# Adding U to the residual on VectorE in every round, and issuing two weight loads with the last slab of the round before

## The chip, the cores and the metric

The kernel runs on one core of one Trainium2 chip. The metric is the device time of one execution in microseconds. Before the change the median of three runs is 1344.67 us (1343.59 to 1345.03).

## What is computed

Two layers of a decoder over 512 tokens of width 1024, in float32. Each layer is a mixer (attention in layer 0, a gated recurrence in layer 1) and then an MLP with a squared ReLU, each behind an RMSNorm and added to the residual stream x. The change lies in the MLP alone, with `w1` of 1024 x 4096 and `w2` of 4096 x 1024:

```python
def squared_relu_mlp(h, w1, w2):
    a = jax.nn.relu(h @ w1)
    return (a * a) @ w2

    ...
        h = rmsnorm(x, norm_gains[layer, 1])
        x = x + squared_relu_mlp(h, mlp_w1[layer], mlp_w2[layer])
```

## The kernel before

The residual stays in SBUF for the whole program, as two tiles `xt[0]` and `xt[1]` (the left and the right half of the columns), each with four blocks of 128 tokens. Float32 products are made of three matmuls: each operand is split into a high part that TensorE takes at full rate and the rest, and high x high, high x low and low x high are added up in PSUM.

**Slabs.** Weights come through a plan, a list of pieces in the order in which TensorE uses them. A piece of `w1` (`full`, 256 columns) is loaded in two halves by SP's DMA queue (`wr`, three buffers, L259). ScalarE casts each half to `wh` (L266), VectorE subtracts to get `wl` (L267). There are two slabs' worth of `wh` and `wl`, and the next slab is always prepared one ahead. So a cast waits until TensorE has left a buffer, and a load waits until the split of an earlier half has freed its `wr`.

**Rounds.** An MLP is four rounds, q = 0 to 3. In a round, four slabs of `w1` (two products of 24 matmuls each, `gemm_w`) give 1024 of the 4096 hidden columns, which `Seven.take` squares and splits. Then a 1024 x 1024 block of `w2` is applied by Strassen's scheme in Winograd's form: seven products of half size instead of eight (`seven_products`). Its four quarters B11, B12, B21, B22 are loaded raw (`load` in `seven`, L288, two DMAs of 512 KB each), and the sums that the scheme needs are made in place, by a negation on ScalarE (`flip`, L294) and an accumulating DMA on GpSimd's queue (L295, L324). Each of the seven slabs is then split by ScalarE (`wh`, L302) and VectorE (`wl`, L303). B12's buffers hold T1 and then T2 later in the round; B12 and B22 share a pool of four buffers (tag R4).

**The seven products** run in this order: a11, s1, a12, s4, s2, s3, a22. Each is two tiles of 12 x 2 matmuls into PSUM, alternating between the pools `mm` and `z`, with two banks each. The first tile's product a11 is kept in `U[t]`, s2's product is added to it (p6, L827), and s3's as well (p7, L832). The residual takes U after s2 (one block) and after s3 (two blocks). The function `back` (L710) is VectorE's addition to `xt`. For the additions of U the kernel before uses `add`: in the last round of an MLP it is `back`, and in the other three a DMA on GpSimd's queue that accumulates into `xt` (L824):

```python
        def add(h, t, u):
            if last:
                back(h, t, u)
            else:
                nc.gpsimd.dma_start(out=xt[h][:, t, :], in_=u, accum_op=ALU.add)
```

After a22 the blocks `xt[0][:, 2 + t]` take that product by `back` as well (p4), which frees its bank of `mm`. The next round's first matmuls (`gemm_w` of the first slab of `w1`) go into the banks of `mm` too.

TensorE's order is that of the program. On the other engines and on the queues a scheduler sets the order when the program is built; each engine and queue then works in order and waits on semaphores.

Of the kernel before, what the change touches and what calls it, by code (L numbers as in the profile page):

```python
# [13 lines left out]
ALU = mybir.AluOpType  # L14
# [3 lines left out]
D = 1024  # L18
# [4 lines left out]
SLAB = 256  # L23
FF = 4 * D
# [35 lines left out]
def trunk(  # L60
# [17 lines left out]
    nc = tc.nc  # L78
# [13 lines left out]
    def sb(tag, shape=(P, S), dt=F32, name=None):  # L92
        pool = gp if tag in "PQ" else ap
        return pool.tile(list(shape), dt, tag=tag, bufs=BUFS[tag], name=name or tag)

    def ps(tag, shape=(P, S), name=None):
        return pp.tile(list(shape), F32, tag=tag, bufs=PB[tag], name=name or f"ps_{tag}")

    def f(t):
        return t.bitcast(F32)  # L100
# [78 lines left out]
    def gain(layer, j, kt):  # L179
# [15 lines left out]
        out=later[:, 3 * P :], in_=later[:, 3 * P :], pattern=[[-1, P]], compare_op=ALU.is_gt,  # L195
# [4 lines left out]
        out=before[:, P:], in_=before[:, P:], pattern=[[1, P]], compare_op=ALU.is_gt,  # L200
# [70 lines left out]
    def seven(w, r0):  # L271

        b = {}

        def rows(i, j, a):
            r = r0 + i * (D // 2) + a * 2 * P
            return w[r : r + 2 * P, j * S : (j + 1) * S].rearrange("(k p) c -> p k c", p=P)

        def load(i, j):

            tag = {(0, 0): "B", (1, 0): "X5", (0, 1): "R4", (1, 1): "R4"}[i, j]
            shape = (P, 10 * P) if tag == "X5" else (P, TT, SLAB)
            b[i, j] = []
            for a in range(2):
                t = sb(tag, shape, name="raw")
                t = t if tag == "X5" else t.rearrange("p t c -> p (t c)")
                t = t[:, : 2 * S].rearrange("p (k c) -> p k c", c=S)
                nc.sync.dma_start(out=t, in_=rows(i, j, a))  # L288
                b[i, j].append(t)

        def flip(at, plus):

            for a in range(2):
                nc.scalar.mul(b[at][a], b[at][a], -1.0)  # L294
                nc.gpsimd.dma_start(out=b[at][a], in_=plus(a), accum_op=ALU.add)  # L295

        def slab(at):
            hi = wp.tile([P, KT // 2, S], F32R, tag="wh", bufs=2, name="wh")
            lo = wp.tile([P, KT // 2, S], F32R, tag="wl", bufs=2, name="wl")
            for a in range(2):  # L300
                c = slice(2 * a, 2 * a + 2)
                nc.scalar.copy(hi[:, c, :], b[at][a])  # L302
                nc.vector.tensor_tensor(  # L303
                    out=lo[:, c, :], in0=b[at][a], in1=f(hi[:, c, :]), op=ALU.subtract
                )
            return hi, lo

        def b12():
            load(0, 1)

        def b11():
            load(0, 0)

        def t1():
            flip((0, 1), lambda a: rows(0, 0, a))
            load(1, 1)

        def b21():
            load(1, 0)

        def slab_t1():
            got = slab((0, 1))
            for a in range(2):
                nc.gpsimd.dma_start(out=b[0, 1][a], in_=rows(1, 1, a), accum_op=ALU.add)  # L324
            flip((0, 0), lambda a: b[0, 1][a])
            return got

        def slab_b21():
            got = slab((1, 0))
            flip((1, 0), lambda a: b[0, 1][a])  # L330
            return got

        slabs = [
            lambda: slab((0, 0)), slab_t1, slab_b21, lambda: slab((1, 1)), lambda: slab((0, 1)),
            lambda: slab((0, 0)), lambda: slab((1, 0)),
        ]
        return [("load", g) for g in (b12, b11, t1, b21)], [("slab", g) for g in slabs]

    class Weights:
        def __init__(self, plan):  # L340
# [24 lines left out]
    def full(w, r0, c0):  # L365
        return (w, r0, KT, c0, SLAB)
# [10 lines left out]

    def plan_mlp(layer):
        got = []
        for q in range(FF // D):  # L380
            loads, slabs = seven(mlp_w2[layer], q * D)
            for c in range(4):
                got += [full(mlp_w1[layer], 0, q * D + c * SLAB), loads[c]]
            got += slabs
        return got

    plan += plan_project(sb_w_o[0]) + plan_mlp(0)
    for hp in range(4):
        plan += [full(hg_w_in[0], 0, n * D + hp * SLAB) for n in range(4)]
    plan += plan_project(hg_w_o[0]) + plan_mlp(1)  # L390
    weights = Weights(plan)

# [33 lines left out]
    xt = [cp.tile([P, TT, S], F32, name=f"xt{h}") for h in range(2)]  # L426
# [282 lines left out]
    def back(h, t, p, op=ALU.add):  # L709
        nc.vector.tensor_tensor(out=xt[h][:, t, :], in0=xt[h][:, t, :], in1=p, op=op)  # L710

    def chain(o, wsl, acts):

        hi, lo = wsl
        n = len(acts)
        for k, (ah, al) in enumerate(acts):
            mm(o, ah, hi[:, k, :], k == 0, False)
            mm(o, ah, lo[:, k, :], False, False)
            mm(o, al, hi[:, k, :], False, k == n - 1)
            yield  # L720
# [75 lines left out]
            }[name]  # L796
            return [[blk(x, at + t) for x in pair] for pair in src]

    def seven_products(A, done, last):


        U = []

        def p1(t, p):
            U.append(sb("AT", name="U"))
            nc.scalar.copy(U[t], p)  # L806
            back(0, t, p)

        def p2(t, p):
            back(0, t, p)  # L810
            done(0, t)

        def p5(t, p):
            back(1, t, p, ALU.subtract)
            back(1, 2 + t, p, ALU.subtract)

        def p3(t, p):
            back(1, t, p)

        def add(h, t, u):  # L820
            if last:
                back(h, t, u)
            else:
                nc.gpsimd.dma_start(out=xt[h][:, t, :], in_=u, accum_op=ALU.add)  # L824

        def p6(t, p):
            nc.vector.tensor_add(U[t], U[t], p)  # L827
            add(1, t, U[t])
            done(1, t)

        def p7(t, p):
            nc.vector.tensor_add(U[t], U[t], p)  # L832
            add(1, 2 + t, U[t])
            done(1, 2 + t)
            add(0, 2 + t, U[t])

        def p4(t, p):
            back(0, 2 + t, p, ALU.subtract)
            done(0, 2 + t)

        steps = [
            ("a11", p1), ("s1", p5), ("a12", p2), ("s4", p3), ("s2", p6), ("s3", p7), ("a22", p4),
        ]
        for n, (name, then) in enumerate(steps):
            wsl = weights.next()
            for t in range(2):
                p = ps("z" if n % 2 else "mm", name="ps_mm")
                yield from chain(p, wsl, A.part(name, t))
                then(t, p)

    def mlp(norm, nxt=None):
        task = line.spawn(norm.finish())
        rounds = FF // D
        for q in range(rounds):
            A = Seven()
            for c in range(4):
                wsl = weights.next()
                if q + c == 0:
                    early = yield from two(wsl, norm)
                    yield [task]  # L860
                for j in range(2):
                    if q + c == 0:
                        p = early[j]
                    else:
                        p = ps("mm")
                        yield from gemm_w(p, wsl, j, norm.acts)
                    u = sb("sq", name="u")
                    nc.vector.scalar_tensor_tensor(  # L868
                        out=u, in0=p, scalar=0.0, in1=norm.R, op0=ALU.max, op1=ALU.mult
                    )  # L870
                    A.take(u)

            def done(h, t):
                if q < rounds - 1:
                    return
                if nxt is None:
                    nc.sync.dma_start(
                        out=out[0, t * P : (t + 1) * P, h * S : (h + 1) * S], in_=xt[h][:, t, :]
                    )
                    return  # L880
                nxt.squares(h, t)
                if t == TT - 1:
                    nxt.turn(h, LAG["x7"] if h else LAG["x"])

            yield from seven_products(A, done, q == rounds - 1)


    def hgrn(norm):
# [292 lines left out]
    for c in range(4):  # L1181
        for j in range(2):
            k = 2 * c + j
            nc.sync.dma_start(
                out=xt[k // 4][:, :, (k % 4) * P : (k % 4 + 1) * P],
                in_=x[0, :, k * P : (k + 1) * P].rearrange("(t p) c -> p t c", p=P),
            )
            if j == 0:
                i = 2 * (c % 2)
                nc.sync.dma_start(  # L1190
                    out=start["raws"][c // 2][:, i : i + 2, :],
                    in_=w0[r0 + 2 * c * P : r0 + 2 * (c + 1) * P, c0 : c0 + SLAB].rearrange(
                        "(k p) c -> p k c", p=P
                    ),
# [61 lines left out]
```

## Time and profile before

| | before |
|---|---|
| median of 3 runs | 1344.67 us |
| profiled execution, its own time | 1343.56 us |
| span of that execution | 1341.9 us |
| mean granted clock of TensorE | 0.981 |
| TensorE busy | 1273.8 us, 95% |
| VectorE busy | 933.5 us, 70% |
| ScalarE busy | 611.6 us, 46% |
| DMA queue of SP (hardware) | 109.22 MB, 25.1% of 16 engines |
| DMA queue of GpSimd (software) | 43.31 MB, 18.4% of 16 engines |
| accumulating DMAs xt<-U | 36 of 256 KB, median 6.0 us to landing |

The profile is of one execution. PE is TensorE, DVE is VectorE, ACT is ScalarE, POOL is GpSimd, SP is the engine that issues most DMAs. In a row of the timeline stand the start and the length in us, the engine, the line, the operation, what is written and read, and in brackets how long the engine was idle before it and who released it. Matmuls are pipelined: the length of one (0.39 us) is more than the distance from one to the next. Layer 0's MLP rounds 1, 2, 3 begin at 403.69, 494.56 and 586.87 us, layer 1's at 1069.20, 1161.98 and 1253.84 us. "Boundary" means the change from one round to the next, so there are three in each MLP, six in all.

### The profile page before, as it was taken

To read this page: it belongs to the slowest core of one execution; us is meant where nothing else is said; L and a number is where in the kernel's file an instruction comes from. 1 tells how busy PE (TensorE), PEld (TensorE's weight loads), DVE (VectorE), ACT (ScalarE), POOL (GpSimd) and SP (SyncE) were. 2 spreads that over 40 slices of the span, in tenths; PEclk is the share of its full clock that TensorE was granted. 3 is DMA by queue.
4 is the path that set the end of the run, shared out by engine and by line. 5 is a ranking of instruction groups with operands and counts; after the bars stand their busy time and mean duration, and the time that the engine had idled before them with its cause. 6 is when DMAs were issued, how large, how long until landed. Compare 5 with 4: busy or idle time off the path is not lost. (4 is left out here: it accounts for less than half of the span.)

```text
span 1341.9 us, 17978 instructions
## 1 busy us (share of the span) xinstructions
PE 1273.8 (95%) x6817; PEld 1079.9 (80%) x6817; DVE 933.5 (70%) x1763; ACT 611.6 (46%) x991; POOL 178.4 (13%) x239
## 2 busy tenths in 40 slices
PE   8999999999989989989999999999999799899798
PEld 7989898778867868768878888888888688687687
DVE  4787687856854846746878888787668457467476
ACT  5555454534733624625552324342446345355262
POOL 1000001000120120210113132232001201203101
PEclk8999999999999989989999999999999899899899
DMA  6312124223394592771532212226424936828615
GB/s 186 95 34 62 38 74 126 95 82 91 73 245 137 94 242 88 165 197 63 96 93 64 90 53 78 63 79 167 132 82 87 256 95 144 217 63 190 186 23 135
DMA packets 109687, 153.68 MB, mean 115 GB/s; under 512 B 5432, under 2 KB 71136, under 8 KB 109600
## 3 DMA queue, kind: packets, MB, share of 16 engines
q1 hardware_dynamic: 91024, 109.22, 25.1%
q0 software_dynamic: 18576, 43.31, 18.4%
q8 instruction: 54, 0.88, 0.3%
q14 instruction: 33, 0.27, 0.1%
HBM read 124.19 MB, written 2.10 MB: 94 GB/s over the span
## 5 line engine op out<-in xcount | busy, mean ns | idle before, releaser
L154 PE MATMUL ps_mm<-xh,wh 128*128 128x512 f32 x592 | 237.9, 402 | 35.5 <-DVE xt L710 35.5
L154 PE MATMUL ps_mm<-xl,wh 128*128 128x512 f32 x592 | 235.2, 397 | 0.0
L154 PE MATMUL ps_mm<-xh,wl 128*128 128x512 f32 x592 | 235.1, 397 | 0.0
L266 ACT CAST wh<-wr 128x1024 fp32r<-128x1024 f32 x134 | 136.4, 1052 | 173.4 <-PE ps_mm L154 123.1
L154 PE MATMUL ps_mm<-wh,xh 128*128 128x256 f32 x592 | 173.5, 293 | 0.0
L154 PE MATMUL ps_mm<-wl,xh 128*128 128x256 f32 x592 | 167.7, 283 | 2.1 <-DVE wl L544 2.1
L267 DVE TENSOR_TENSOR wl<-wr,wh 128x1024 fp32r<-128x1024 f32 x134 | 162.1, 1231 | 9.1 <-ACT wh L266 8.9
L154 PE MATMUL ps_mm<-wh,xl 128*128 128x256 f32 x592 | 167.6, 283 | 0.0
L154 PEld LDWEIGHTS ps_mm<-xh,wh 128*128 128x128 f32 x592 | 114.5, 193 | 61.4 <-issue 37.9
L303 DVE TENSOR_TENSOR wl<-raw,wh 128x1024 fp32r<-128x1024 f32 x112 | 132.7, 1220 | 37.4 <-ACT wh L302 37.3
L710 DVE TENSOR_TENSOR xt<-xt,ps_mm 128x512 f32<-128x512 f32 x128 | 86.0, 682 | 83.1 <-PE ps_mm L154 47.3
L154 PEld LDWEIGHTS ps_mm<-xh,wl 128*128 128x128 f32 x592 | 114.0, 193 | 24.4
L154 PEld LDWEIGHTS ps_mm<-xl,wh 128*128 128x128 f32 x592 | 114.3, 193 | 23.3
L302 ACT CAST wh<-raw 128x1024 fp32r<-128x1024 f32 x112 | 111.4, 1047 | 44.0 <-PE ps_mm L154 40.4
L154 PEld LDWEIGHTS ps_mm<-wh,xh 128*128 128x128 f32 x592 | 113.4, 192 | 4.1 <-issue 3.6
L154 PEld LDWEIGHTS ps_mm<-wl,xh 128*128 128x128 f32 x592 | 113.5, 192 | 2.8 <-DVE wl L544 2.3
L154 PEld LDWEIGHTS ps_mm<-wh,xl 128*128 128x128 f32 x592 | 113.5, 192 | 0.0
L324 POOL DMA_DIRECT2D raw<-in_mlp_w_dram x16 | 19.5, 1247 | 546.5 <-DVE wl L303 546.0
L868 DVE SCALAR_TENSOR_TENSOR u<-ps_mm,R 128x512 f32<-128x512 f32 x60 | 41.4, 689 | 66.2 <-PE ps_mm L154 66.2
L294 ACT ACTIVATE raw<-raw 128x1024 f32<-128x1024 f32 x48 | 50.7, 1059 | 38.7 <-DMA raw<-in_mlp_w_dram 38.7
L667 DVE TENSOR_TENSOR_SCAN sn<-sn,later 128x128 f32<-128x128 f32 (+3 forms) x64 | 51.2, 816 | 8.4 <-ACT sn L664 7.4
L154 PE MATMUL ps_mm<-wl,s31h 128*128 128x512 f32 x128 | 51.7, 404 | 4.2 <-DVE wl L303 4.2
(236 smaller groups left out, 2543.8 us busy)
## 6 DMA issues: line engine op xcount, KB each, us to landing
raw<-in_mlp_w_dram SPq DMA_DIRECT2D x64, 512.0 KB, 7.5
wr<-in_mlp_w_dram SPq DMA_DIRECT2D x64, 512.0 KB, 4.7
raw<-in_mlp_w_dram POOLq DMA_DIRECT2D x32, 512.0 KB, 6.3
raw<-raw POOLq DMA_DIRECT2D x32, 512.0 KB, 5.8
wr<-in_hg_w_in_dram SPq DMA_DIRECT2D x32, 512.0 KB, 3.8
wr<-in_sb_w_qkv_dram SPq DMA_DIRECT2D x22, 512.0 KB, 3.8
xt<-U POOLq DMA_DIRECT2D x36, 256.0 KB, 6.0
wr<-in_sb_w_o_dram SPq DMA_DIRECT2D x8, 512.0 KB, 3.9
```

What stands on the lines that cost most here:

```text
L154: nc.tensor.matmul(o, lhsT=lhsT, rhs=rhs, start=start, stop=stop, **kw)
L266: nc.scalar.copy(hi[:, c, :], raw)
L267: nc.vector.tensor_tensor(out=lo[:, c, :], in0=raw, in1=f(hi[:, c, :]), op=ALU.subtract)
L294: nc.scalar.mul(b[at][a], b[at][a], -1.0)
L302: nc.scalar.copy(hi[:, c, :], b[at][a])
L303: nc.vector.tensor_tensor(out=lo[:, c, :], in0=b[at][a], in1=f(hi[:, c, :]), op=ALU.subtract)
L324: nc.gpsimd.dma_start(out=b[0, 1][a], in_=rows(1, 1, a), accum_op=ALU.add)
L667: nc.vector.tensor_tensor_scan(out=rev, data0=rev, data1=later[:, S - W :][:, ::-1], initial=1.0, op0=ALU.mult, op1=ALU.max,)
L710: nc.vector.tensor_tensor(out=xt[h][:, t, :], in0=xt[h][:, t, :], in1=p, op=op)
L868: nc.vector.scalar_tensor_tensor(out=u, in0=p, scalar=0.0, in1=norm.R, op0=ALU.max, op1=ALU.mult)
```

## The change

U is added to the residual by `back`, so by VectorE, in all rounds: `add` and its DMA go, 36 of them (six at each boundary). And the load steps of a round are put together differently. Before: B12, B11, then the negation and accumulation that make T1 together with the load of B22, then B21, one after each `w1` slab. After: B12 and B22 are one step, `early`, which stands ahead of the last slab of the round before (in an MLP's first round, behind its first `w1` slab), then B11, B21 and T1 stand between the `w1` slabs.

```diff
-        def b12():
+        def early():
             load(0, 1)
-
-        def b11():
-            load(0, 0)
+            load(1, 1)
 
         def t1():
             flip((0, 1), lambda a: rows(0, 0, a))
-            load(1, 1)
-
-        def b21():
-            load(1, 0)
...
-        return [("load", g) for g in (b12, b11, t1, b21)], [("slab", g) for g in slabs]
+        steps = (early, lambda: load(0, 0), lambda: load(1, 0), t1)
+        return [("load", g) for g in steps], [("slab", g) for g in slabs]
...
     def plan_mlp(layer):
         got = []
-        for q in range(FF // D):
-            loads, slabs = seven(mlp_w2[layer], q * D)
-            for c in range(4):
-                got += [full(mlp_w1[layer], 0, q * D + c * SLAB), loads[c]]
-            got += slabs
+        rounds = [seven(mlp_w2[layer], q * D) for q in range(FF // D)]
+        for q, ((early, *loads), slabs) in enumerate(rounds):
+            w1 = [full(mlp_w1[layer], 0, q * D + c * SLAB) for c in range(4)]
+            got += w1[:1] + ([] if q else [early])
+            for slab, step in zip(w1[1:], loads):
+                got += [step, slab]
+            got += slabs[:-1] + [r[0][0] for r in rounds[q + 1 : q + 2]] + slabs[-1:]
         return got
...
-        def add(h, t, u):
-            if last:
-                back(h, t, u)
-            else:
-                nc.gpsimd.dma_start(out=xt[h][:, t, :], in_=u, accum_op=ALU.add)
-
         def p6(t, p):
             nc.vector.tensor_add(U[t], U[t], p)
-            add(1, t, U[t])
+            back(1, t, U[t])
             done(1, t)
 
         def p7(t, p):
             nc.vector.tensor_add(U[t], U[t], p)
-            add(1, 2 + t, U[t])
+            back(1, 2 + t, U[t])
             done(1, 2 + t)
-            add(0, 2 + t, U[t])
+            back(0, 2 + t, U[t])
```

How this moves instructions is seen in the order in which they stand on each engine. VectorE before, at the end of the first round of layer 0, from s2's U to the splits of the second `w1` slab (`xt_99` is `xt[0]`, `xt_100` is `xt[1]`):

```order
L827 TENSOR_TENSOR U<-U,ps_mm 128x512 x2
L303 TENSOR_TENSOR wl<-raw,wh 128x1024 x2
L832 TENSOR_TENSOR U<-U,ps_mm 128x512 x2
L267 TENSOR_TENSOR wl<-wr,wh 128x1024 x2
L710 TENSOR_TENSOR xt_99<-xt_99,ps_mm 128x512 x2
L267 TENSOR_TENSOR wl<-wr,wh 128x1024 x2
```

VectorE now, at the same place, from the addition of s2's second U on (lines are three to nine lower in the changed text, so `back` is L707):

```order
L707 TENSOR_TENSOR xt_100<-xt_100,U 128x512
L303 TENSOR_TENSOR wl<-raw,wh 128x1024 x2
L823 TENSOR_TENSOR U<-U,ps_mm 128x512
L707 TENSOR_TENSOR xt_100<-xt_100,U 128x512
L707 TENSOR_TENSOR xt_99<-xt_99,U 128x512
L823 TENSOR_TENSOR U<-U,ps_mm 128x512
L707 TENSOR_TENSOR xt_100<-xt_100,U 128x512
L707 TENSOR_TENSOR xt_99<-xt_99,U 128x512
L267 TENSOR_TENSOR wl<-wr,wh 128x1024
L707 TENSOR_TENSOR xt_99<-xt_99,ps_mm 128x512
L267 TENSOR_TENSOR wl<-wr,wh 128x1024
L707 TENSOR_TENSOR xt_99<-xt_99,ps_mm 128x512
```

Each U is followed by its additions, six per boundary, and a22's first `back` stands behind one split of the first `w1` slab instead of two. Nothing else moves on VectorE; the orders of TensorE and ScalarE do not change, and on GpSimd's queue only the DMAs xt<-U are gone.

SP's queue before, at the boundary from the first to the second round of layer 0. The numbers tell the loads apart: raw_4101 and 4103 are the next round's B12, 4265 and 4267 its B22, 4181 and 4183 its B11, 4367 and 4369 its B21; wr_4107 and 4111 are the halves of its second `w1` slab:

```order
L259 DMA wr_4107<-in_mlp_w1_dram 128x4x256
L288 DMA raw_4101<-in_mlp_w2_dram 128x2x512
L288 DMA raw_4103<-in_mlp_w2_dram 128x2x512
L288 DMA raw_4265<-in_mlp_w2_dram 128x2x512
L288 DMA raw_4267<-in_mlp_w2_dram 128x2x512
L288 DMA raw_4181<-in_mlp_w2_dram 128x2x512
L288 DMA raw_4183<-in_mlp_w2_dram 128x2x512
L288 DMA raw_4367<-in_mlp_w2_dram 128x2x512
L288 DMA raw_4369<-in_mlp_w2_dram 128x2x512
L259 DMA wr_4111<-in_mlp_w1_dram 128x4x256
```

SP's queue now, at the same place. Here raw_4025 and 4027 are B12, 4029 and 4031 B22, 4109 and 4111 B11, 4189 and 4191 B21; wr_4115 and 4119 are the halves of the second `w1` slab:

```order
L259 DMA wr_4115<-in_mlp_w1_dram 128x4x256
L288 DMA raw_4025<-in_mlp_w2_dram 128x2x512
L288 DMA raw_4027<-in_mlp_w2_dram 128x2x512
L288 DMA raw_4029<-in_mlp_w2_dram 128x2x512
L288 DMA raw_4031<-in_mlp_w2_dram 128x2x512
L288 DMA raw_4109<-in_mlp_w2_dram 128x2x512
L288 DMA raw_4111<-in_mlp_w2_dram 128x2x512
L288 DMA raw_4189<-in_mlp_w2_dram 128x2x512
L288 DMA raw_4191<-in_mlp_w2_dram 128x2x512
L259 DMA wr_4119<-in_mlp_w1_dram 128x4x256
```

Only the names have changed: the loads of B12, B22, B11 and B21 stand in this order, behind the first half of the second `w1` slab, in both.

4 lines of the change are left out of this document (2 added, 2 removed).

## The prediction

> **What bounds the kernel now.** I read the page first, for the engine that is busiest, then the waits of TensorE, then the chain of waits, and then, round by round, TensorE's own timeline and its clock.
>
> ```profile
> PE 1273.8 (95%) x6817; PEld 1079.9 (80%) x6817; DVE 933.5 (70%) x1763; ACT 611.6 (46%) x991; POOL 178.4 (13%) x239
> ```
>
> TensorE (PE) is the bound: it is busy 95% of the 1341.9 us span. So a change to VectorE (DVE) or to the DMA queues is worth what it takes out of TensorE's idle time, or out of its slow time. TensorE's waits, by total (engine, line, who was waited for: us, times, longest):
>
> ```profile
> PE ps_mm L154 <- DVE xt L710: 36.5, 7, 7.3
> PE ps_mm L154 <- DVE wl L303: 4.2, 6, 0.8
> PE ps_mm L154 <- ACT wh L302: 2.0, 4, 0.9
> ```
>
> The first row is by far the largest wait of TensorE: for VectorE's `back` (L710), which adds a product in PSUM to the residual. TensorE's timeline shows where. These are the first matmuls of rounds 1, 2 and 3 of each MLP, with the idle time ahead of each in brackets:
>
> ```profile
> 403.69 0.77 PE L154 MATMUL ps_mm<-xh,wh 128*128 128x512 f32 x1 [6.43 <-DVE xt L710]
> 494.56 0.76 PE L154 MATMUL ps_mm<-xh,wh 128*128 128x512 f32 x1 [4.72 <-DVE xt L710]
> 586.87 0.77 PE L154 MATMUL ps_mm<-xh,wh 128*128 128x512 f32 x1 [5.94 <-DVE xt L710]
> 1069.20 0.77 PE L154 MATMUL ps_mm<-xh,wh 128*128 128x512 f32 x1 [6.47 <-DVE xt L710]
> 1161.98 0.58 PE L154 MATMUL ps_mm<-xh,wh 128*128 128x512 f32 x1 [4.69 <-DVE xt L710]
> 1253.84 0.77 PE L154 MATMUL ps_mm<-xh,wh 128*128 128x512 f32 x1 [7.26 <-DVE xt L710]
> ```
>
> Six boundaries, 6.43 + 4.72 + 5.94 + 6.47 + 4.69 + 7.26 = **35.5 us** idle. TensorE wants one of the two `mm` banks of PSUM there, which the last product, a22, has left full until VectorE's `back` empties it. The chain of waits through the fifth boundary (start, length, what) tells why that is late:
>
> ```profile
> 1145.68 0.69 DVE U L827
> ...
> 1146.66 7.57 DMA xt<-U
> ...
> 1154.36 0.70 DVE U L832
> ...
> 1155.88 5.17 DMA xt<-U
> ...
> 1161.14 0.70 DVE xt L710
> ```
>
> Two accumulating DMAs in series. The s3 product's addition into U (L832) may not overwrite U before the DMA that read it has landed, and a22's `back` (L710) may not touch the residual before the DMA into the same tile has landed. VectorE's waits say the same for all six boundaries:
>
> ```profile
> DVE U L832 <- DMA xt<-U: 38.5, 12, 5.8
> DVE xt L710 <- DMA xt<-U: 35.6, 12, 4.7
> ```
>
> An idle TensorE also loses its clock. Windows of 6 us from each restart, one clean stretch, and one 8 us window which is spoken of below (length, busy and matmuls counted, granted clock, DMA share, GB/s):
>
> ```profile
> 403.69:409.69 6.00, 6.00 (x18) 0.65 0.74 203
> 494.56:500.56 6.00, 6.00 (x15) 0.55 0.80 224
> 586.87:592.87 6.00, 6.00 (x16) 0.56 0.82 226
> 1069.20:1075.20 6.00, 6.00 (x18) 0.65 0.74 210
> 1161.98:1167.98 6.00, 6.00 (x20) 0.72 0.77 215
> 1253.84:1259.84 6.00, 6.00 (x18) 0.67 0.71 205
> 1260.00:1330.00 70.00, 70.00 (x309) 1.00 0.36 83
> 1143.00:1151.00 8.00, 6.81 (x22) 0.79 0.96 187
> ```
>
> The clean stretch gives 70.00 / 309 = 0.2265 us per matmul, so 26.5 in 6 us. The six windows hold 105 matmuls where 6 x 26.5 = 159 would fit: 54 x 0.2265 = **12.2 us** lost to the clock behind the gaps. (By the granted clock it is 6 us x the sum of what each lacks to 1.00, 2.20, so 13.2 us; I take the count.) The Trainium skill (TensorE: Matmul & The Clock Gate, "HAM oscillation") has an idle gap longer than about 3.4 us followed by a stretch at half rate whose penalty is half its length. With one window of 3.4 us behind each gap that would be 1.7 us a gap, 10.2 us in all, and the saving below 45.7 us; the counted windows show more, so the count decides.
>
> **The change, part by part.**
>
> *The 36 accumulating DMAs go.* With them go both waits in the table of VectorE's waits, and so the chain above. What is late next at the boundary has to be worked out, because VectorE now does the 36 additions itself, 6 ahead of each boundary. The trace of before has that work already: the last round of each MLP adds U on VectorE. In that of layer 0:
>
> ```profile
> 658.57 0.68 DVE L827 TENSOR_TENSOR U<-U,ps_mm 128x512 f32<-128x512 f32 x1
> 659.29 0.69 DVE L710 TENSOR_TENSOR xt<-xt,U 128x512 f32<-128x512 f32 x1
> ...
> 664.30 0.68 DVE L832 TENSOR_TENSOR U<-U,ps_mm 128x512 f32<-128x512 f32 x1
> 665.01 1.29 DVE L710 TENSOR_TENSOR xt<-xt,U 128x512 f32<-128x512 f32 x2
> 666.29 0.69 DVE L832 TENSOR_TENSOR U<-U,ps_mm 128x512 f32<-128x512 f32 x1
> 667.01 1.29 DVE L710 TENSOR_TENSOR xt<-xt,U 128x512 f32<-128x512 f32 x2
> 668.22 1.22 DVE L267 TENSOR_TENSOR wl<-wr,wh 128x1024 fp32r<-128x1024 f32 x1
> ```
>
> An addition takes 0.69 us. A U with one addition takes 0.72 + 0.69 = 1.4 us, a U with two 666.29 - 664.30 = 2.0 us. VectorE's added work is 36 x 0.69 = 24.8 us, 4.1 us a boundary. Does it fit? I replay the fifth boundary, the one with the latest start, with the changed order of VectorE. Four more rows give the split of a slab and TensorE's and the queue's times:
>
> ```profile
> 1143.40 2.36 DVE L303 TENSOR_TENSOR wl<-raw,wh 128x1024 fp32r<-128x1024 f32 x2 [5.66 <-ACT wh L302]
> ```
>
> ```profile
> 1151.89 2.00 ACT L266 CAST wh<-wr 128x1024 fp32r<-128x1024 f32 x2 [5.67 <-PE ps_mm L154]
> 1157.33 1.04 ACT L266 CAST wh<-wr 128x1024 fp32r<-128x1024 f32 x1 [3.44 <-PE ps_mm L154]
> 1165.85 1.05 ACT L266 CAST wh<-wr 128x1024 fp32r<-128x1024 f32 x1 [7.48 <-DMA wr<-in_mlp_w_dram]
> ```
>
> ```profile
> 1158.21 20.15 SPq L259 DMA_DIRECT2D wr<-in_mlp_w_dram  x6
> ```
>
> ScalarE's first two casts each wait for TensorE to leave a buffer of wh, so s3 ends at 1151.9 and a22 at 1157.3. VectorE starts U at 1145.7. Two pairs of U and addition, 2.8: 1148.5. The two splits of a22's slab, 2.4: 1150.9, wanted at 1151.9. Two groups of U with two additions, 4.0: 1154.9. One split of the first w1 slab, 1.2: 1156.1. Then a22's first `back`, 0.7: the bank is free at **1156.8**, and TensorE wants it at 1157.3. So the bank is there 0.5 us ahead, and the gap of 4.69 us goes altogether. The second split ends at 1158.0; TensorE comes to that half 12 matmuls x 0.2265 = 2.7 us after 1157.3. I take the other boundaries as alike: no wait for wl or wh ahead of s3 is longer than 0.8 or 0.9 us.
>
> Next comes the second half of the second w1 slab, which is loaded only when the first split has freed its buffer. In before, issue at 1158.21 and cast at 1165.85 are 7.6 us apart. With the issue at 1156.1 the cast starts at 1163.7 and the split ends about 1.05 + 1.2 later, at 1166.0. TensorE, without its gap, begins that slab after 48 matmuls, 10.9 us, at 1168.2. Hidden by 2.2 us; were that cover gone, each us of it would cost 6 us.
>
> *The pool queue.* GpSimd issues six DMAs fewer per boundary; its others keep their order. Only VectorE waited for them, by the two rows above. Worth nothing beyond those.
>
> *The move of the loads.* In the text, B12 and B22 of the next round now stand ahead of the round's last slab. On SP's queue, by the order shown, they stand where they stood, behind the same three w1 loads and ahead of the other quarters. ScalarE's and TensorE's orders are also unchanged. I cost this at nothing. What it could touch is the short wait just ahead of the s3 product, the second and third rows of TensorE's waits: 4.2 + 2.0 = 6.2 us in all. There ScalarE is held up by the next B12:
>
> ```profile
> 1140.16 1.06 ACT L294 ACTIVATE raw<-raw 128x1024 f32<-128x1024 f32 x1 [6.63 <-DMA raw<-in_mlp_w_dram]
> ```
>
> It stays, since the load still waits for the same split. Bounds: from 6.2 us gained to some us lost (first rival).
>
> **The sum** is 35.5 + 12.2 = **47.7 us**. The profiled execution took 1343.56 us (span 1341.9), 1.1 us below the median of 1344.67 and just below the lowest of the three runs shown. Against itself it comes to 1295.9; against the median **1297.0 us**, which is my forecast.
>
> **The rivals.**
>
> *The clock falls at the short wait too.* The 8 us window above holds the short wait of the fifth boundary. TensorE is busy 6.81 us in it, and the granted clock is 0.79: (1 - 0.79) x 8 = 1.7 us lost, although no wait there is longer than 0.9 us. Of the six boundaries only this one has it, so the length of the wait does not settle it, and with shorter rounds other boundaries may be hit: all six would be 5 x 1.7 = 8.5 us more, 1305.5 us. (The Trainium skill, on the same page under "What's actually happening", has the window in which activity is measured run freely; by that rule the moment at which a stall falls decides, which agrees with one in six.) For it: the short waits remain. Against it: five of six had none. Chance 0.13.
>
> *The moved loads do land earlier.* If B12 came before ScalarE asks for it, the 6.2 us and the 1.7 us at the fifth boundary would go too: 1297.0 - 7.9 = 1289.1. Against it: same place on the queue. Chance 0.07.
>
> *VectorE is late.* The slack at the bank is 0.5 us. If the 4.1 us of additions found no cover at all, 3.6 us would remain at each boundary: 6 x 3.6 = 21.6 us, 1318.6. Against it: VectorE sat idle just there, waiting in L832 for the DMAs that go, 38.5 us over six boundaries, 6.4 us each. Chance 0.06.
>
> *Slower: the early loads block w1.* SP issues in order, and a load that waits for its buffer holds up what is behind it. If the four early loads stood ahead of the three w1 loads, w1's would wait for them. One early load takes 10.64 us to land in the chain:
>
> ```profile
> 1130.66 10.64 DMA raw<-in_mlp_w_dram
> ```
>
> Two such landings in series would put the w1 split 21.3 us later, at 1187.3. TensorE wants that half at 1168.2 + 2.7 = 1170.9: a stall of 16.4 us at each boundary, 98 us in all against 47.7 gained, so 1395. It decides for slower from 8 us a boundary on (47.7 / 6). The order speaks against it. Chance 0.03.
>
> **How the numbers follow.** Forecast as worked 0.70, the clock 0.13, earlier loads 0.07, VectorE late 0.06, w1 blocked 0.03; 0.01 that something else eats the gain just so. The first three cases lie between 1289 and 1306, to which I add the 1.1 us by which the profiled run and the median differ: 1288 to 1307. A measurement of this kernel can tell about 0.2%, 2.7 us, from no change. Faster 0.96, same 0.01, slower 0.03.
>
> **What would show it.** Right, if the changed profile has no row of TensorE waiting 4 us and more for `back`, no accumulating DMA into xt, a granted clock near 1.00 in the first 6 us of each round, and the short waits ahead of s3 still there, about 6 us. Wrong, if a wait of several us stands at the first matmul of a round for a slab (wh, wl) or for `back`; if the mean granted clock does not rise; or if ScalarE's wait for the next B12 has changed.

## The result and the profile after

| | before | after |
|---|---|---|
| median | 1344.67 us | 1297.17 us (1294.92 to 1300.2, 3 runs) |
| profiled execution, its own time | 1343.56 us | 1297.17 us |
| span of that execution | 1341.9 us | 1295.5 us |
| mean granted clock of TensorE | 0.981 | 0.996 |

The ratio of the two is 0.965, 95% interval 0.9618 to 0.9683: 47.5 us less by the medians, 46.4 us by the spans. In the changed kernel `back` is L707, p6 is L818 and p7 is L823.

From the page after, the engines' busy time and the row of GpSimd's DMA queue (packets, MB, share of 16 engines):

```profile
PE 1259.6 (97%) x6817; PEld 1069.5 (83%) x6817; DVE 956.2 (74%) x1799; ACT 611.6 (47%) x991; POOL 146.7 (11%) x203
...
q0 software_dynamic: 13392, 33.87, 14.8%
```

TensorE does the same 6817 matmuls in 14.2 us less busy time, so its clock was better. VectorE has 36 instructions more and 22.7 us more busy time. The 36 DMAs are gone: 9.44 MB and 36 instructions of POOL less. TensorE's waits after:

```profile
PE ps_mm L154 <- DVE xt L707: 4.9, 7, 1.0
...
PE ps_mm L154 <- DVE wl L303: 3.8, 6, 0.8
...
PE ps_mm L154 <- ACT wh L302: 1.1, 3, 0.6
```

The wait for `back` fell from 36.5 us to 4.9, and the short waits ahead of s3 from 6.2 us to 4.9. The wait for `back` has not gone altogether: the page's group of the first matmuls, and the fifth boundary in TensorE's timeline, show a rest of 0.6 to 0.7 us at each of the six boundaries.

```profile
L154 PE MATMUL ps_mm<-xh,wh 128*128 128x512 f32 x592 | 232.6, 393 | 4.0 <-DVE xt L707 4.0
```

```profile
1125.72 0.47 PE L154 MATMUL ps_mm<-xh,wh 128*128 128x512 f32 x1 [0.67 <-DVE xt L707]
```

The same windows as before, 6 us from the restart at each boundary (length, busy time and count of PE, PEld, DVE, ACT and POOL, then granted clock, DMA share, GB/s):

```profile
398.36:404.36 6.00, 6.00 (x27) 4.96 (x28) 4.21 (x5) 1.51 (x2) 0.00 (x0) 1.00 0.75 232
483.27:489.27 6.00, 6.00 (x27) 4.97 (x28) 4.22 (x5) 1.46 (x2) 0.00 (x0) 1.00 0.77 239
566.96:572.96 6.00, 6.00 (x26) 4.96 (x27) 4.19 (x5) 1.47 (x2) 0.00 (x0) 1.00 0.79 240
1041.06:1047.06 6.00, 6.00 (x26) 4.95 (x27) 4.19 (x5) 1.47 (x2) 0.00 (x0) 1.00 0.79 238
1125.72:1131.72 6.00, 6.00 (x26) 4.96 (x27) 4.19 (x5) 1.47 (x2) 0.00 (x0) 1.00 0.79 243
1209.33:1215.33 6.00, 6.00 (x27) 4.97 (x28) 4.22 (x5) 1.48 (x2) 0.00 (x0) 1.00 0.76 229
```

They hold 159 matmuls, where before they held 105, at a granted clock of 1.00 throughout.

**Where the time went.** Gaps 35.5 - 4.0 = 31.5 us; the clock behind them 12.2; the clock at the fifth boundary's short wait (0.79 before) 1.7; the short waits 6.2 - 4.9 = 1.3. Together 46.7 us, and the spans differ by 46.4. A second sum goes by TensorE alone: all the rows of its waits fall by 31.9 us (63.7 to 31.8) and its busy time by 14.2, together 46.1. The 1.7 us belong to that one execution of the kernel before rather than to the change, as is shown at the end.

VectorE's timeline at the fifth boundary shows what is late now. It has no wait for a DMA any more, but it works without a break from 1112.7 until the bank is free:

```profile
1114.99 0.68 DVE L818 TENSOR_TENSOR U<-U,ps_mm 128x512 f32<-128x512 f32 x1
...
1117.64 2.35 DVE L303 TENSOR_TENSOR wl<-raw,wh 128x1024 fp32r<-128x1024 f32 x2
...
1122.55 1.29 DVE L707 TENSOR_TENSOR xt<-xt,U 128x512 f32<-128x512 f32 x2
1123.76 1.22 DVE L267 TENSOR_TENSOR wl<-wr,wh 128x1024 fp32r<-128x1024 f32 x1
1124.90 0.68 DVE L707 TENSOR_TENSOR xt<-xt,ps_mm 128x512 f32<-128x512 f32 x1
...
1129.63 1.23 DVE L267 TENSOR_TENSOR wl<-wr,wh 128x1024 fp32r<-128x1024 f32 x1 [1.18 <-ACT wh L266]
```

### The profile page after: what moved, and what is told of

Read it like the earlier page. It is cut to its first block, busy times and chain, and to the rows that moved or that the text cites. A ratio compares the mean times of both kernels' runs of the same rounds, so it can differ in the third digit from the quotient of the medians.

```text
span 1295.5 us, 17920 instructions
## 1 busy us (share of the span) xinstructions
PE 1259.6 (97%) x6817; PEld 1069.5 (83%) x6817; DVE 956.2 (74%) x1799; ACT 611.6 (47%) x991; POOL 146.7 (11%) x203
## 3 DMA queue, kind: packets, MB, share of 16 engines
q0 software_dynamic: 13392, 33.87, 14.8%
## 5 line engine op out<-in xcount | busy, mean ns | idle before, releaser
L154 PE MATMUL ps_mm<-xh,wh 128*128 128x512 f32 x592 | 232.6, 393 | 4.0 <-DVE xt L707 4.0
L154 PE MATMUL ps_mm<-xh,wl 128*128 128x512 f32 x592 | 230.5, 389 | 0.0
L154 PE MATMUL ps_mm<-xl,wh 128*128 128x512 f32 x592 | 230.5, 389 | 0.0
L154 PEld LDWEIGHTS ps_mm<-xh,wh 128*128 128x128 f32 x592 | 111.2, 188 | 28.7 <-issue 6.3
L154 PEld LDWEIGHTS ps_mm<-xh,wl 128*128 128x128 f32 x592 | 111.1, 188 | 23.3
L154 PEld LDWEIGHTS ps_mm<-xl,wh 128*128 128x128 f32 x592 | 111.2, 188 | 22.3
L707 DVE TENSOR_TENSOR xt<-xt,ps_mm 128x512 f32<-128x512 f32 x128 | 86.0, 682 | 47.9 <-PE ps_mm L154 47.7
L859 DVE SCALAR_TENSOR_TENSOR u<-ps_mm,R 128x512 f32<-128x512 f32 x60 | 41.4, 690 | 63.7 <-PE ps_mm L154 63.7
L294 ACT ACTIVATE raw<-raw 128x1024 f32<-128x1024 f32 x48 | 50.7, 1058 | 36.4 <-DMA raw<-in_mlp_w_dram 36.3
L1021 DVE COPY_PREDICATED sc<-masks,ps_s 128x32 f32<-128x32 uint8 (+9 forms) x176 | 46.5, 298 | 13.0 <-PE ps_s L154 11.0
```

The source lines that it names most:

```text
L154: nc.tensor.matmul(o, lhsT=lhsT, rhs=rhs, start=start, stop=stop, **kw)
L859: nc.vector.scalar_tensor_tensor(out=u, in0=p, scalar=0.0, in1=norm.R, op0=ALU.max, op1=ALU.mult)
L1021: nc.vector.copy_predicated(out=o, mask=mask.rearrange("p (g w) -> p g w", g=g)[:, None].to_broadcast([P, 2, g, w]), data=data.rearrange(" ...
```

## The experiments

The theory was that of the prediction: at each boundary VectorE waits for two accumulating DMAs in series, TensorE waits for VectorE, and its clock falls behind the gap; the moved loads do nothing. The rivals: the loads carry part of the gain; the DMA traffic itself, not VectorE's waits for it, costs the time; the slow clock has another cause than the idle time. Each run has its own runs of the kernel before on the same chip, with medians of 1343.19 us (for each half of the change alone, the 18 matmuls, and `back` ahead of U), 1341.44 (for each cut alone, the copy, and the negation on GpSimd), 1342.84 (for both cuts, the 30 matmuls, and both additions together) and 1345.44 (for the last kernel). Times from different chips are compared by their ratios.

### Each half of the change alone

The kernel before with `add` always as `back`, loads left where they were:

```diff
         def add(h, t, u):
-            if last:
-                back(h, t, u)
-            else:
-                nc.gpsimd.dma_start(out=xt[h][:, t, :], in_=u, accum_op=ALU.add)
+            back(h, t, u)
```

> The kernel before with U added by VectorE in all rounds, and the loads as they were. If the accumulating DMAs are the whole cause, this is the changed kernel: 1297 us, a ratio to before of 0.965, six waits for back of 0.7 us and a granted clock that no boundary pulls down. If the moved loads had a part in the gain, it is slower than 1300 us, and TensorE's waits ahead of s3 (wl L303, wh L302) are about 6.2 us as in before, against 4.9 us in the changed kernel.

Measured: 1296.47 us, ratio 0.9652 (0.9638 to 0.9667). TensorE's waits are those of the changed kernel: 4.9 us for `back`, and 3.9 and 1.1 us ahead of s3. And the changed kernel with the DMAs put back, so that only the loads are moved:

```diff
-            back(1, t, U[t])
+            add(1, t, U[t])
...
-            back(1, 2 + t, U[t])
+            add(1, 2 + t, U[t])
...
-            back(0, 2 + t, U[t])
+            add(0, 2 + t, U[t])
```

> The changed kernel with the accumulating DMAs back, so that only the load steps are moved. If the place on SP's queue decides, nothing changes: 1344.7 us, within 0.2% of before, and 35 us of waits for back. If the earlier place in the plan brings B12 earlier, it falls by up to 7.9 us, to 1337 us.

Measured: 1343.7 us, ratio 0.9998 (0.9986 to 1.001). TensorE's wait for `back` is all there:

```profile
PE ps_mm L154 <- DVE xt L707: 40.3, 7, 7.8
```

The additions are the whole gain; moving the loads is worth nothing that can be measured. The order of instructions on every engine says the same: with the additions alone it is that of the changed kernel, with the loads alone that of the kernel before.

### Which wait on the DMAs holds the bank

First cut: the 12 additions to `xt[0]` that share a tile with a22's `back` go to VectorE, the other 24 DMAs stay.

```diff
             add(1, 2 + t, U[t])
             done(1, 2 + t)
-            add(0, 2 + t, U[t])
+            back(0, 2 + t, U[t])
```

> The kernel before with only the two additions of U to the left half's lower blocks on VectorE (12 of the 36 DMAs go): a22's back no longer waits for a DMA, L832 still waits for the first ones. If the chain is two DMAs in series, of which the second overlaps VectorE's splits, little goes: L832 starts as late as before, and two additions and two splits stand between it and a22's back, so about 1 us less a boundary, 1337 us. If the DMA ahead of a22's back is what counts, the waits for back fall under 1 us and the time to 1297 us.

Measured: 1334.98 us, ratio 0.9946 (0.9926 to 0.9966). VectorE's wait in L832 stays, and TensorE's for `back` is 31.2 us:

```profile
DVE U L832 <- DMA xt<-U: 33.6, 11, 5.7
```

Second cut: s3's sum goes to a tile of its own, so that L832 need not wait for the DMA that reads U; all 36 DMAs stay.

```diff
-            nc.vector.tensor_add(U[t], U[t], p)
-            add(1, 2 + t, U[t])
+            V = sb("sq", name="V7")
+            nc.vector.tensor_add(V, U[t], p)
+            add(1, 2 + t, V)
             done(1, 2 + t)
-            add(0, 2 + t, U[t])
+            add(0, 2 + t, V)
```

> The kernel before with s3's sum written into a tile of its own instead of over U (all 36 DMAs stay): L832 no longer waits for the first DMAs, a22's back still waits for the last ones. If the first DMA of the chain is the dearer one, as 7.57 us against 5.17 us and the work behind L832 say, the waits for back fall to 0.6 to 2 us a boundary, 4 to 12 us in all, and with them part of the 12.2 us of clock: 1305 to 1320 us. If the second DMA decides alone, the time stays near 1344 us.

Measured: 1341.74 us, ratio 0.9997 (0.9985 to 1.0009): a miss, it gained nothing. The wait in L832 is gone, but VectorE now waits in `back` instead. From VectorE's waits:

```profile
DVE xt L710 <- DMA xt<-V: 60.2, 12, 8.2
```

From the chain of waits at its fifth boundary, U's sum and the DMA that a22's `back` waits for:

```profile
1144.05 0.74 DVE U L827 x2
...
1149.03 10.34 DMA xt<-V
```

It starts 5.0 us after U's sum, where before there lay 10.2 us between the two (1145.68 to 1155.88). And yet it lands 15.3 us after that sum (1159.37), and before it was 15.4 (1161.05), because it takes 10.34 us and not 5.17. Over the whole run the 24 DMAs from V take 10.8 us at the median, where the 36 of before took 6.0:

```profile
xt<-V POOLq DMA_DIRECT2D x24, 256.0 KB, 10.8
```

The DMA share beside it gives the likely reason. Two windows at the fifth boundary of before, then the same stretch with the second cut, then two windows of the changed kernel:

```profile
1150.00:1158.00 8.00, 7.29 (x32) 5.66 (x31) 2.33 (x3) 2.68 (x3) 2.40 (x4) 1.00 1.08 309
1158.00:1166.00 8.00, 4.02 (x11) 3.18 (x12) 2.00 (x3) 0.52 (x2) 1.08 (x2) 0.79 1.10 243
```

```profile
1149.00:1157.00 8.00, 6.64 (x30) 5.14 (x28) 3.05 (x3) 3.04 (x3) 2.97 (x4) 1.00 1.09 274
```

```profile
1120.00:1128.00 8.00, 7.33 (x33) 5.76 (x32) 7.93 (x11) 2.70 (x3) 0.00 (x0) 1.00 0.60 205
1128.00:1136.00 8.00, 8.00 (x37) 6.64 (x36) 3.22 (x5) 2.09 (x3) 0.00 (x0) 1.00 0.66 199
```

With the accumulating DMAs there, the share is 1.08 to 1.10, so the 16 engines are all taken. In the changed kernel it is 0.60 and 0.66 at this place (0.99 a little earlier, from 1115 to 1123, under the weight loads alone). A DMA that is issued earlier would then only share the engines with more others. In this run the 12 DMAs from U are slower too, 9.0 us at the median. This reading is argued, not shown: the share was 1.08 in before as well, where the DMA took 5.17 us, and whether the DMAs share the engines or GpSimd's queue is not separated.

Then both cuts at once:

```diff
-            nc.vector.tensor_add(U[t], U[t], p)
-            add(1, 2 + t, U[t])
+            V = sb("sq", name="V7")
+            nc.vector.tensor_add(V, U[t], p)
+            add(1, 2 + t, V)
             done(1, 2 + t)
-            add(0, 2 + t, U[t])
+            back(0, 2 + t, V)
```

> The kernel before with both links of the chain cut at once: s3's sum goes to a tile of its own, V (so no wait for the DMA that reads U), and the 12 additions to xt[0] are done by VectorE (so a22's back has no DMA to wait for). The 24 accumulating DMAs into xt[1] stay. Each cut alone gave 0 and 6 us. If what counts is whether VectorE waits for any of these DMAs, the two cuts together bring what neither brings alone: no wait for back longer than 1 us, and 1341 to 1344 less 45 to 48 us, so 1294 to 1299. If the traffic itself costs TensorE time (late loads, 24 of 36 DMAs still there), at most a third of the gain comes: 1325 and more.

Measured: 1294.9 us, ratio 0.9636 (0.9603 to 0.9668), the whole gain, with 24 of the 36 DMAs still there, at 8.2 and 8.5 us to landing (medians of those from U and from V). VectorE at the fifth boundary reaches the `back` that frees the bank (1121.96) with nothing to wait for but s3:

```profile
1116.33 0.69 DVE L710 TENSOR_TENSOR xt<-xt,V 128x512 f32<-128x512 f32 x1
1118.36 0.69 DVE L833 TENSOR_TENSOR V<-U,ps_mm 128x512 f32<-128x512 f32 x1 [1.33 <-PE ps_mm L154]
1119.08 0.69 DVE L710 TENSOR_TENSOR xt<-xt,V 128x512 f32<-128x512 f32 x1
1119.69 2.35 DVE L267 TENSOR_TENSOR wl<-wr,wh 128x1024 fp32r<-128x1024 f32 x2
1121.96 0.68 DVE L710 TENSOR_TENSOR xt<-xt,ps_mm 128x512 f32<-128x512 f32 x1
```

The DMA share there is as high as in before, and TensorE has no gap (two windows, in the order of the windows above):

```profile
1112.00:1120.00 8.00, 8.00 (x30) 6.35 (x28) 6.60 (x10) 2.33 (x3) 3.31 (x4) 0.79 1.03 247
1120.00:1128.00 8.00, 8.00 (x37) 6.63 (x36) 4.55 (x5) 1.41 (x2) 0.19 (x1) 1.00 1.09 304
```

So one cut is worth 6 us, the other nothing, and both together 48 us. Each of VectorE's two waits alone keeps the bank nearly as long as both do; only with the second gone as well does the gap close. And the traffic as such costs TensorE nothing that can be seen here: the DMAs may be slow as long as nobody waits for them. (The clock of 0.79 in the first window stands behind the short waits ahead of s3; more on it at the end.)

### What the slow clock costs by itself

The gap was filled: matmuls that nobody reads, into a bank of the pool `tr`, at the start of rounds 1 to 3. VectorE stays as late as it is. Twice, with 18 and with 30 of them:

```diff
             A = Seven()
+            if q:
+                idle = ps("tr", name="ps_idle")
+                for n in range(18):
+                    mm(idle, ones_r, norm.acts[n % KT][0], True, True)
```

> The kernel before with 18 matmuls of 512 columns at each of the six boundaries, whose result nobody reads. They run while TensorE waits for back (18 x 0.2265 = 4.1 us of a gap of 4.7 to 7.3 us) and shorten no wait. If the clock behind the gaps is a cost of its own, the time falls although work was added: by the 12.2 us that were counted, to 1332.5 us, less where the 0.6 to 3.2 us of idle time that are left still pull the clock down. If only the waiting counts, it stays at 1344.7 us.

Measured: 1340.25 us, ratio 0.9986 (0.9968 to 1.0003). A miss: 18 matmuls, 4.1 us, were too few, because gaps of 1.9 to 4.1 us remained. The second and third boundaries in TensorE's timeline, and 8 us from the start of each gap:

```profile
494.90 0.47 PE L154 MATMUL ps_mm<-xh,wh 128*128 128x512 f32 x1 [2.02 <-DVE xt L710]
586.42 0.47 PE L154 MATMUL ps_mm<-xh,wh 128*128 128x512 f32 x1 [1.90 <-DVE xt L710]
```

```profile
492.80:500.80 8.00, 5.98 (x20) 4.74 (x20) 2.50 (x4) 1.04 (x1) 0.00 (x0) 0.79 0.90 209
584.40:592.40 8.00, 6.10 (x27) 4.99 (x27) 2.13 (x3) 1.05 (x1) 0.00 (x0) 1.00 0.88 209
```

Behind the gap of 2.02 us the clock fell (0.79 over 8 us, which is 3.4 us at half rate), behind that of 1.90 us it did not; at the four other boundaries, with gaps of 2.2 to 4.1 us, it fell as well. The Trainium skill (TensorE: Matmul & The Clock Gate, "What's actually happening") has activity measured in a window of about 3.4 us that runs freely. The length of 3.4 us agrees with it. Its "HAM oscillation" section names gaps above about 3.4 us as the dangerous ones; the gap of 2.02 us does not agree.

With 30 matmuls, 30 x 0.2265 = 6.8 us a boundary:

> The kernel before with 30 matmuls that nobody reads at each boundary, 6.8 us at full clock, instead of the 18 that left 2 to 3 us of idle time; what ends the gap, VectorE's back, stays as late as it is. If the slow clock behind a gap comes from the idle time and costs 12 us on top of it, then no slow stretch is left behind five of the six boundaries (the longest gap, 7.3 us, keeps an idle rest below 1 us), and the kernel takes 1331 to 1336 us (the gaps that are shorter than the filling give back some: 2.1, 0.9, 0.3 and 2.1 us, 5 us in all). If the slow stretches have another cause (the DMA traffic beside them, say), they stay, and it takes 1344 to 1349.

Measured: 1332.35 us, ratio 0.9923 (0.9897 to 0.9948). VectorE waits for the DMAs as long as before, but the clock stays at 1.00 behind every boundary (waits of VectorE; 6 us behind the filling at the first, fifth and sixth boundary):

```profile
DVE U L832 <- DMA xt<-U: 40.0, 12, 5.9
DVE xt L710 <- DMA xt<-U: 36.3, 12, 4.4
```

```profile
403.36:409.36 6.00, 6.00 (x28) 4.99 (x27) 2.25 (x3) 1.05 (x1) 0.00 (x0) 1.00 0.74 215
...
1152.72:1158.72 6.00, 6.00 (x28) 4.95 (x28) 2.43 (x3) 1.06 (x1) 0.00 (x0) 1.00 0.71 198
1243.22:1249.22 6.00, 5.64 (x25) 4.57 (x25) 1.66 (x3) 1.05 (x1) 0.00 (x0) 1.00 0.86 232
```

The filling adds 180 x 0.2265 = 40.8 us of work, TensorE's waits, all of its rows together, fall by 36.3 us (63.7 to 27.4), and still the kernel takes 10.5 us less. So the clock gave back 40.8 - 36.3 + 10.5 = 15.0 us, or 16.5 by the spans of the two profiled executions, from which the waits are. Of these 16.5 us some 1.7 are not of the boundaries: in before the clock also falls ahead of the MLP, from 248 to 256 us (0.85 and 0.72 in two windows of 4 us), and in this execution it does not. That leaves 14.8 us. The prediction's count for the gaps is 12.2, and with the 1.7 at the short wait 13.9. The DMA share there is as high as in the windows of before (0.71 to 0.86), and the clock no longer falls, so it is the idle time that brings it down, not the traffic.

### What is left: 0.67 us a boundary, and the short waits

First, a22's `back` ahead of the two additions of U to the same block:

```diff
         def p7(t, p):
             nc.vector.tensor_add(U[t], U[t], p)
             back(1, 2 + t, U[t])
             done(1, 2 + t)
-            back(0, 2 + t, U[t])

         def p4(t, p):
             back(0, 2 + t, p, ALU.subtract)
+            back(0, 2 + t, U[t])
             done(0, 2 + t)
```

> The changed kernel with the two additions of U to the left half's lower blocks moved behind a22's back, so that VectorE does 1.3 us less ahead of the bank's release. If the 0.66 us that are left at each boundary (4.0 us in all) are VectorE's queue, they go: 1293.2 us. If it is then the split of the first w1 slab that TensorE waits for, the wait only changes its name and the time stays at 1297 us.

Measured: 1298.63 us, ratio 0.9668 (0.9645 to 0.969): a miss, no gain over the changed kernel. VectorE at the fifth boundary:

```profile
1126.63 0.69 DVE L707 TENSOR_TENSOR xt<-xt,U 128x512 f32<-128x512 f32 x1
1127.24 2.35 DVE L267 TENSOR_TENSOR wl<-wr,wh 128x1024 fp32r<-128x1024 f32 x2
1129.52 0.68 DVE L707 TENSOR_TENSOR xt<-xt,ps_mm 128x512 f32<-128x512 f32 x1
```

The scheduler put both splits of the next `w1` slab ahead of a22's `back`, where the changed kernel has one. What two additions gave, the second split took back.

Then a22's product was copied out of PSUM by ScalarE in rounds 0 to 2, and `back` reads the copy, so that the bank no longer waits for VectorE (`last` is true in the last round, where nothing follows):

```diff
         def p4(t, p):
+            if not last:
+                e = sb("sq", name="e4")
+                nc.scalar.copy(e, p)
+                p = e
             back(0, 2 + t, p, ALU.subtract)
```

> The changed kernel with a22's product copied out of PSUM by ScalarE in rounds 0 to 2, so that the bank is free 0.6 us after the product instead of behind VectorE's queue. If the 0.66 us at each boundary are VectorE's queue, the 4.0 us go: 1293.2 us. If the split of the first w1 slab is as late as the bank, half of it or nothing goes: 1295 to 1297 us.

Measured: 1290.18 us, ratio 0.961 (0.9594 to 0.9627). The six waits are gone, and the time fell by 3 us more than was expected, for a reason that is not shown. One wait of 1.0 us at another place is left:

```profile
PE ps_mm L154 <- DVE xt L707: 1.0, 1, 1.0
```

Against the short waits ahead of s3, T1's negation went from ScalarE to GpSimd in the changed kernel:

```diff
-        def flip(at, plus):
+        def flip(at, plus, pool=False):
...
-                nc.scalar.mul(b[at][a], b[at][a], -1.0)
+                if pool:
+                    nc.gpsimd.tensor_scalar_mul(b[at][a], b[at][a], -1.0)
+                else:
+                    nc.scalar.mul(b[at][a], b[at][a], -1.0)
...
-            flip((0, 1), lambda a: rows(0, 0, a))
+            flip((0, 1), lambda a: rows(0, 0, a), True)
```

> The changed kernel with the negation that starts T1 on GpSimd instead of ScalarE. If the short waits ahead of s3 (4.9 us left: wl 3.8, wh 1.1) come from ScalarE standing in that negation until the next B12 has landed, they go, and the time falls by 4 to 5 us to 1292.5 us. If GpSimd and VectorE hinder one another, or T1 comes late, it rises above 1297 us.

Measured: 1292.62 us, ratio 0.9628 (0.9612 to 0.9644). The short waits are gone, and the six waits for `back` too, but a new one of 5.3 us has come, for GpSimd in layer 1's mixer, with a clock of 0.51 in the 4 us behind it (904 to 908), 2 us more:

```profile
PE kt L158 <- POOL kk L997: 5.3, 1, 5.3
```

That the waits for `back` went as well shows what the 0.67 us hung on: VectorE's late start. In the changed kernel VectorE sits idle for 5.12 us until 1112.71, where ScalarE's cast of s3's slab comes, behind the negation. With the negation away from ScalarE, VectorE begins U's first sum at 1109.87 and TensorE wants the bank at 1122.27, 12.4 us later; in the changed kernel there are 10.1 us between them. GpSimd and VectorE do hinder one another: beside the negations at 1107.15 and 1111.71, two splits of VectorE took 3.20 us instead of 2.36 and an addition of U 1.89 instead of 0.69. Here VectorE had the room for it.

Both together:

> The changed kernel with the two additions that each gained on it: a22's product copied out of PSUM by ScalarE ahead of back (7 us less than the changed kernel alone, the six waits of 0.66 us gone and some more) and T1's negation on GpSimd (4.6 us less, the short waits ahead of s3 gone). If they act at different places they add up: 1297.2 - 7.0 - 4.6 = 1285.6 us, 1284 to 1288. If both only take away the same waits (the copy loads ScalarE, which the negation frees), it stays at the better of the two, 1290 to 1293.

Measured: 1294.32 us, ratio 0.9634 (0.961 to 0.9658). The copy alone had 0.961, the negation alone 0.9628: no gain of the copy on top of the negation can be told, and the negation takes away the six waits by itself. The new wait is explained by GpSimd's timeline:

```profile
900.79 3.54 POOL L295 TENSOR_SCALAR raw<-raw 128x1024 f32<-128x1024 f32 x1 [4.98 <-DMA raw<-in_mlp_w_dram]
904.31 0.61 POOL L1001 TENSOR_TENSOR kk<-kk,tot 128x256 f32<-128x256 f32 x1
```

A negation of round 0 stands on GpSimd's queue while its load is under way, ahead of the recurrence's work (`kk`) for which TensorE waits. So the last kernel leaves round 0's negations on ScalarE:

```diff
-            flip((0, 1), lambda a: rows(0, 0, a), True)
+            flip((0, 1), lambda a: rows(0, 0, a), r0 > 0)
```

> The kernel with both additions, but T1's negation goes to GpSimd only in rounds 1 to 3 of each MLP; in round 0 it stays on ScalarE. Reason: in the kernel with both, one negation of round 0 of the second MLP stands on GpSimd's queue while its load is still under way (5.0 us), ahead of the gated recurrence's work there, and TensorE waits 5.3 us for that. If this is why the two gains did not add up, that wait goes, the short waits ahead of s3 stay gone in six of eight rounds, and the kernel takes 1286 us (1284.5 to 1288), less than with the copy alone (1290.2). If the two additions take away the same waits, it stays at 1289 to 1292.

Measured: 1285.02 us (1281.23 to 1286.33), ratio 0.9554 (0.9536 to 0.9573). The wait for `kk` is gone with it, which settles the cause of that wait, and this version is faster than both kernels. That the two additions add up is not shown by it: of the some 10 us by which it is below the kernel with the negation alone (ratio 0.9628), the wait of 5.3 us and the 2 us of slow clock behind it account for 7.3, and this kernel without the copy was not run.

## Why the prediction was right, point by point

**The bound and the gaps: right.** TensorE's wait for `back` was what the change took away, 31.5 of the 35.5 us, and the additions do it alone.

**Why the gap was there: partly wrong.** The prediction read the chain of waits as two DMAs in series. The waits are both real, but their sum is not the length of the gap: with the wait in L832 cut away, the DMA ahead of a22's `back` takes 10.34 us instead of 5.17 and lands as late as before, beside a DMA share of 1.09. The change removes both waits at once, so the forecast did not suffer.

**VectorE's slack of 0.5 us: wrong.** It was 0.67 us late at this boundary, and 0.62 to 0.68 at the others: 4.0 us of the forecast gain did not come. The replay was not too fast for VectorE. It had the bank free 11.1 us after the start of U's first sum (1145.7 to 1156.8), and VectorE needed 10.6 (1114.99 to 1125.58). It was TensorE that was taken as too slow: it wanted the bank 11.6 us after U in the replay, and 10.1 us after the change (1125.72 - 0.67 - 1114.99). In before, the fifth boundary is the one at which TensorE ran s3 at half clock (the window with 0.79), which gave VectorE 1.5 us. The step that failed is "I take the other boundaries as alike". The fifth, the one "with the latest start", was the easiest. The trace of before has the others too. At the first, U's first sum starts here:

```profile
387.19 1.28 DVE L827 TENSOR_TENSOR U<-U,ps_mm 128x512 f32<-128x512 f32 x2
```

TensorE wants the bank at 403.69 - 6.43 = 397.26, 10.1 us later, and at the second, third, fourth and sixth boundary it is 10.1 us as well. Against the 11.1 us of the replay, that is 1.0 us late.

**The clock, 12.2 us: right.** Filling the gaps gave 14.8 us for the slow clock at the boundaries, by the spans, against 13.9 by the prediction's two counts. The 1.7 us at the fifth boundary's short wait, which the sum left standing, came on top: its window was not slow in this execution. It and the 1.3 us of shorter waits make up for most of the 4.0 us. That the median falls within 0.2 us of the forecast is therefore luck: 4.0 us failed to come, 3.0 came that were not in the sum, and the three runs range over 5.3 us.

**w1's second half: right, with a wrong size.** The prediction had it hidden by 2.2 us, from 7.6 us between issue and cast. After, the split ends at 1129.63 + 1.23 = 1130.9, and TensorE begins that slab 10.9 us after 1125.72, at 1136.6: hidden by 5.7 us. The load was issued at 1125.01 and the cast began at 1128.54, 3.5 us later instead of 7.6, beside a DMA share of 0.60 to 0.66 instead of 1.08 to 1.10.

**GpSimd's queue and the moved loads, both at nothing: right**, by the runs with each half alone and with both cuts.

**The rivals.** No load came earlier to any effect, and none was blocked: ScalarE's wait for loads ahead of its negations, the next B12 among them, is 36.3 us in all after the change and 38.7 before, and its casts wait 15.3 us for loads of `w1`, where it was 49.0. VectorE was late, by 0.67 us and not 3.6.

Whether the clock falls at the short waits is a matter of the execution. In the eleven profiled executions that have short waits ahead of s3, it fell three times behind them, each time at the fifth boundary: in before, with the second cut, and with both cuts. There the two waits, with one matmul between them, come to 1.59 to 1.64 us. It did not fall behind a pair of 1.69 us (first cut, first boundary), nor behind any that comes to 1.40 us or less. The kernel with the loads alone has the order of before, and its clock did not fall there. The three runs of the changed kernel point the same way: their spans of 1293.2, 1295.5 and 1298.5 us go with mean clocks of 0.997, 0.996 and 0.994, but only the middle one has a trace that shows where.

**The signs that were named: met, with one in doubt.** No single wait for `back` is longer than 1.0 us, but its row adds up to 4.9, so "no row of 4 us and more" holds for the waits and not for their sum. No accumulating DMA into `xt` is left, the clock is 1.00 behind each boundary, and the short waits are still there, 4.9 us and not about 6.

## What to carry to other kernels

A chain of waits names what came last, not what the time depends on: before a gap is put down to one of two waits on DMAs, ask whether the other would hold it as long, and read the DMA share beside it. Here, at a share of 1.09, a DMA that was issued 5 us earlier landed no earlier. And an addition of 0.69 us on an engine with idle time beat a DMA of 6.0 us where somebody waited for it; where nobody waited, the DMA cost nothing that could be seen. When an engine's slack is replayed from a trace, replay it at a place where the bound engine runs at full clock, or the slack will be too large by what the slow clock gave; and where the trace has six such places, read all six.

## What the hardware showed

- Idle time of TensorE of 2.02 us was followed by 3.4 us at half rate, 1.90 us was not, nor 0.67 us. Two waits close together did it at 1.59 to 1.64 us in sum (three times) and not at 1.69 us (once). So the length alone does not decide; that the moment does is likely, and not shown.
- Work that nobody reads, in place of the idle time, made the kernel 10.5 us faster.
- An accumulating DMA of 256 KB took 6.0 us at the median when the six of a boundary were spread out by waits, and 10.8 us where the last four of a boundary were issued 3 to 6 us behind the first two, without waiting for them.
- Beside GpSimd's negation VectorE was slower: 1.89 us for an addition that otherwise takes 0.69.
- GpSimd's negation of 128 x 1024 took 3.54 us in the row above; ScalarE's took 1.06 us in the row that the prediction shows.
